# Mixture-of-experts blocks: adding a block's sums in steps between the next block's products, and the gather on both sides of the transposes

## The chip, the cores and the metric

The kernel runs on one core of a Trainium2 chip. The metric is the device time of one execution in microseconds (us). A core has a matrix engine (PE, with its weight loads PEld), a vector engine (DVE), an activation engine (ACT), a general engine (POOL), and SP, which here does little else than start DMA transfers. Each engine runs its own list of instructions in order; semaphores between them make one wait for another.

## The reference

Two layers, each a sequence mixer followed by a hierarchical mixture of experts (MoE) with 32 experts of 1024 x 1024 (gate and up) and 512 x 1024 (down) weights. All of it is in float32. What matters here is the MoE:

```python
def hier_moe(h, w_group, b_group, w_expert, b_expert, w_gate_up, w_down):
    g_logits = hf @ w_group + b_group                       # 4 groups
    g_sel = jnp.argmax(g_logits, -1)                        # top-1 group
    g_gate = take(softmax(g_logits), g_sel)
    e_logits = take((hf @ w_expert + b_expert).reshape(n_tok, 4, 8), g_sel)
    top_p, top_i = lax.top_k(jax.nn.softmax(e_logits, -1), 2)
    top_w = top_p / jnp.sum(top_p, -1, keepdims=True) * g_gate[:, None]
    # ... each (token, choice) goes to its expert e:
    def expert_block(args):
        xb, e = args
        gu = xb @ w_gate_up[e]                              # 1024 -> 2 x 512
        return (jax.nn.silu(gu[:, :512]) * gu[:, 512:]) @ w_down[e]   # 512 -> 1024
    return jnp.sum(out[dest].reshape(n_tok, 2, -1) * top_w[..., None], axis=1)

for i in range(2):                                          # layer 0: SSD mixer, layer 1: retention mixer
    x = layer_norm(ALPHA * x + g1 * (mixer(modulate(x)) @ out_w))     # layer 0: ctx the same way
    tokens = modulate(x, sh2, sc2)                          # layer 0: 256 latent + 256 context tokens; layer 1: 256
    ffn = hier_moe(tokens, ...)
    x = layer_norm(ALPHA * x + g2 * ffn)
```

Each MoE reads all 32 experts' weights once, 6 MB for each expert.

## The kernel before

The two mixers and the two MoEs follow each other. In a MoE (class `MoE`) every expert has a fixed number of slots for the tokens that chose it: 32, 64 or 96. Experts are worked off in blocks of 128 slots, by the loop in `pairs()`: a narrow block holds four experts of 32 slots, a wide one two of 64, a full one an expert of 96 and one of 32. Layer 0 (512 tokens, `nt` = 4 tiles of 128) has twelve blocks, here called p0 to p11: wide, wide, narrow, full, narrow, wide, wide, narrow, wide, wide, narrow, wide. Layer 1 (256 tokens, `nt` = 2) has ten. Blocks are grouped in twos for the gather.

For a block the loop issues, in this order, before the change:

- `gate_up`: for k = 0 to 7 the gate products (pg) and up products (pu) of each expert, L1839. An expert's tokens lie on 32 or 64 of PE's columns, so products of different experts stand side by side on the array (the rows show the tile as 128\*32 or 128\*64). Behind it tanh and two multiplications give th (L1844, L1848, L1849).
- `scatter_oh`: pb (L1809), from which DVE makes the one-hot matrix os that puts slots back to tokens.
- `ahead`: the block's share of the gather for the next group. One `part` is `gather` (px, L1778, 16 matmuls in layer 0 and 8 in layer 1, then copies into xT); each block of a group of two does two parts. The second block also does `weights`: `slot_w` (pw, L1794), the routing weight of each slot.
- `hidden_T`: four transposes of th (ph, L1856), copied to hT by ACT (L1858).
- `add`: the previous block's output is put back to tokens: for two halves u and `nt` token tiles two matmuls (pc, L1886), then DVE multiplies by the gate (L1911) and adds to the sum (L1912). That is 16 pc in layer 0 and 8 in layer 1, eight or four such steps.
- `down`: the down products (pd, L1868). `weighted` then scales them and splits them in two (ACT L1878, DVE L1879), which the next `add` reads.

Around p0 `ahead` stands behind `after` instead (LATE = 0). Behind block p5 in layer 0 and p4 in layer 1 (`REST`) the last block is added at once and `rest()` follows: a loop under `If` (L2087) over blocks for tokens beyond an expert's slots. Its count is zero for these inputs.

Inside an engine the order is not that of the code: these calls go through the framework's scheduler, which reorders matmuls of neighbouring steps where their data is there; so the pieces of order below are of the final programs. Weights come through a ring of 1 MB matrices in the pools A, B, E, F and X: `Ring.emit` (L175) starts a transfer (L186, on SP's queue) when the next matrix of a fixed plan finds a free slot, and a slot is free again when `done` has seen the last product that reads it, for a gate and up matrix behind every second k. SP issues strictly in the plan's order, so one slot that is late holds all later ones.

Of the kernel before, what the change touches and what calls it, by code (L numbers as in the profile page):

```python
# [27 lines left out]
EPS = 1e-5  # L28
LN = ("mix", "ffn")
REST = (5, 4)  # L30
FIXED, FULL = 4, 4

SLOTS = ([64] * 4 + [96] + [64] * 10 + [32] * 17, [32] * 4 + [96] + [64] * 6 + [32] * 21)
# [7 lines left out]
def const_layout():  # L41
# [3 lines left out]
    def add(name, a):  # L45
        parts.append((name, np.ascontiguousarray(a, dtype=np.float32)))

    add("ident", np.eye(128))
    add("r8", np.tile(np.arange(8, 0, -1), (128, 1)))
    add("i96", np.tile(np.arange(96), (128, 1)))  # L50
    add("s64", (i % 64)[:, None])
    e = np.arange(32)
# [157 lines left out]
def col(S, name, a=0, b=None):  # L210
    o, w = CL[name]
    return S.c[:, o + a:o + (w if b is None else b)]
# [1249 lines left out]
LATE = 0  # L1462
# [39 lines left out]
class MoE:  # L1502
# [397 lines left out]
            G.tensor_tensor(o, o, ln[:, 1024:], OP.add)  # L1900
        S.ring.done(("mix", self.layer))

    def add(self, os_, ys, n):
        V = self.S.nc.vector
        for u in range(2):
            for i in range(self.nt):
                pc = self.ps([P, 512], "pc", "cb")
                self.scattered(pc, os_, ys, n, i, u)
                c = slice(u * 512, (u + 1) * 512)
                t = self.wk2.tile([P, 512], F32, name="tl", bufs=2)  # L1910
                V.tensor_tensor(t, pc, self.gate(i)[:, c], OP.mult)  # L1911
                V.tensor_tensor(self.acc(i)[:, c], self.acc(i)[:, c], t, OP.add)  # L1912


    def pairs(self):
        S, order, groups = self.S, self.order, self.groups
        i96, s32, s64, s96 = (col(S, n) for n in ("i96", "s32", "s64", "s96"))
        xT, ws, G = {}, {}, self.G
        last = len(order) - 1

        def one_hots(g):
            runs = []
            for e in (e for p in groups[g] for e in order[p]):
                if runs and e == runs[-1][1] and self.slots(e) == self.slots(runs[-1][0]):
                    runs[-1][1] += 1
                else:
                    runs.append([e, e + 1])
            return self.gather_oh([(self.pos[:, :, a:b], self.slots(a)) for a, b in runs], i96)

        def weights(g):  # L1930
            for j, p in enumerate(groups[g]):
                ws[p] = self.slot_w(G[g], P * j, order[p])

        def start(g):
            for p in groups[g]:
                xT[p] = self.wk.tile([P, 8, P], F32, name="xT", bufs=3)

        def part(g, q, nb=2):
            self.gather(G[g], [xT[p] for p in groups[g]], q, nb)

        def ahead(p, g):
            own = groups[g - 1]
            for q in range(4)[slice(4 * own.index(p) // len(own), 4 * (own.index(p) + 1) // len(own))]:
                part(g, q)
            if p == own[-1]:
                weights(g)
        start(0)
        prev = None
        later = self.rest_of_route()

        def first(k):
            if k < 2 or k % 2 == 0:
                part(0, k if k < 2 else k // 2, 1 if k < 2 else 2)
            if k in ROUTE_K:
                next(later)

        def after(th, W, os_, w, end=False):
            nonlocal prev
            hT = self.hidden_T(th)
            if prev is not None:  # L1960
                self.add(*prev)
            pd = self.down(W, hT)
            prev = (os_, pd, w) if end else (os_, self.weighted(pd, w), 2)
        for p, places in enumerate(order):
            g = next(j for j, own in enumerate(groups) if p in own) + 1
            new = g < len(groups) and p == groups[g - 1][0]
            experts = {e: Expert(S, self.layer, e) for e in places}
            tiles = self.tiles_of(places)
            W = [(experts[e], w) for e, w in tiles]
            if new and p:  # L1970
                G[g] = one_hots(g)
            th = self.gate_up(W, xT[p], None if p else first)
            if p == 0:
                G[1] = one_hots(1)
                self.spread_rows()
            widths = [w for _, w in tiles]
            os_ = self.scatter_oh([(S.id2[:, e:e + 1], w) for e, w in tiles],
                                  s64 if widths[0] == 64 else s32 if len(experts) == 4 else s96)
            if g < len(groups):
                if p == 0:  # L1980
                    weights(0)
                    self.blocks()
                    self.base()
                if new:
                    start(g)
                if p > LATE:
                    ahead(p, g)
            after(th, W, os_, ws[p], p == last)
            if g < len(groups) and p <= LATE:
                ahead(p, g)  # L1990
            if p == REST[self.layer]:
                self.add(*prev)
                prev = None
                self.rest()
        return prev
# [286 lines left out]
```

## Time and profile before

| What | Value |
|---|---|
| runs, median (lowest to highest) | 2008.51 us (2006.31 to 2010.71), 3 runs |
| the profiled execution | 2005.95 us, span 2004.2 us |
| PE busy | 1769.8 us, 88% |
| PEld, DVE, ACT, POOL busy | 1002.5, 953.0, 489.4, 456.8 us |
| DMA moved | 543.84 MB, mean 271 GB/s |
| chain that ended last | DMA 8%, PE 2%, DVE 1% of the span |

The first MoE lies between about 620 and 1110 us, the second between about 1540 and 1985 us. In the page's forty slices the DMA engines' share is at 0.9 or more in most of these two stretches and much lower in the mixers, where PE is the busy engine. A window row gives, for a stretch from A to B in us, each engine's busy time with the count of instructions, the clock that PE was granted (1.00 is full), the mean share of time in which the core's DMA engines were busy, and what they moved; a share of 1.02 to 1.03 is what a full queue shows here. A timeline row gives start, duration, engine, line, operation, output and inputs by name, shape and count; in brackets is how long the engine had stood idle and what released it. A row of waits gives who waited for whom: total us, how many times, the longest. One float32 product shows as two passes in the timeline (x2).

### The profile page before, as it was taken

What the parts mean: (1) busy time and instruction counts of PE and PEld (TensorE: products, weight loads), DVE (VectorE), ACT (ScalarE), POOL (GpSimd) and SP (SyncE); (2) the same over time, 40 slices, a digit from 0 to 9 for tenths busy, and PEclk for the clock granted to TensorE, in tenths of its full rate; (3) what the DMA queues carried; (4) which work ended last, traced back from release to release, by engine and by line L of the source; (5) the groups of instructions that cost most, each with busy time, mean ns of one, the idle gap of its engine ahead of it and who ended that gap; (6) DMA issues with size and microseconds to landing.
All of it is one profiled execution on the core that took longest, in us unless ns stands there. A gap on an engine that the chain in (4) does not pass through costs nothing. (4 is left out here: it accounts for less than half of the span.)

```text
span 2004.2 us, 23517 instructions
## 1 busy us (share of the span) xinstructions
PE 1769.8 (88%) x9021; PEld 1002.5 (50%) x9021; DVE 953.0 (48%) x1685; ACT 489.4 (24%) x827; POOL 456.8 (23%) x275
## 2 busy tenths in 40 slices
PE   6899999999986999998999789988897998788886
PEld 3665666666764433332332488776873432123221
DVE  3847575765696434433243566474454432103112
ACT  2555454543212100000000233232232100000000
POOL 2343425343345000000000243454551100000000
PEclk8999999999997999999999899999997999989998
DMA  7423323336735999999999744474367999999996
GB/s 284 150 99 116 126 95 136 111 111 220 275 109 223 371 399 399 373 383 401 409 406 368 290 149 146 155 263 145 113 255 294 409 409 409 409 375 407 409 409 242
DMA packets 138022, 543.84 MB, mean 271 GB/s; under 512 B 10320, under 2 KB 10832, under 8 KB 125360
## 3 DMA queue, kind: packets, MB, share of 16 engines
q1 hardware_dynamic: 137328, 541.80, 69.9%
q8 instruction: 73, 1.20, 0.2%
q10 hardware_dynamic: 576, 0.48, 0.1%
q14 instruction: 45, 0.37, 0.0%
HBM read 537.00 MB, written 5.24 MB: 271 GB/s over the span
## 5 line engine op out<-in xcount | busy, mean ns | idle before, releaser
L441 POOL TENSOR_TENSOR wl<-ringA,wh 128x1024 fp32r<-128x1024 f32 x116 | 290.0, 2512 | 812.0 <-ACT wh L440 794.0
L440 ACT ACTIVATE wh<-ringA 128x1024 fp32r<-128x1024 f32 x118 | 124.3, 1058 | 225.5 <-PE pin L720 61.0
L720 PE MATMUL pin<-u,wh 128*128 128x512 f32 x304 | 132.0, 434 | 0.0
L1868 PE MATMUL pd<-ringB,hT 128*32 128x512 f32 (+1 forms) x472 | 123.0, 617 | 6.0 <-ACT hT L1858 4.5
L721 PE MATMUL pin<-u,wl 128*128 128x512 f32 x304 | 127.4, 419 | 0.0
L719 PE MATMUL pin<-u,wh 128*128 128x512 f32 x304 | 126.9, 417 | 0.0
L1879 DVE SCALAR_TENSOR_TENSOR yh<-pd,ws,yh 128x512 fp32r<-128x512 f32 x40 | 30.0, 751 | 198.1 <-ACT yh L1878 196.2
L1839 PE MATMUL pg<-ringE,xT 128*32 128x512 f32 (+1 forms) x312 | 110.4, 609 | 7.7 <-DMA ringE<-in_moe_w_gate_up_dram 7.2
L1839 PE MATMUL pu<-ringE,xT 128*32 128x512 f32 (+1 forms) x312 | 110.6, 609 | 3.6 <-DMA ringE<-in_moe_w_gate_up_dram 3.6
L1844 ACT ACTIVATE th<-pg 128x512 f32<-128x512 f32 x22 | 13.1, 597 | 402.9 <-PE pg L1839 392.8
L1848 DVE SCALAR_TENSOR_TENSOR th<-th,pg 128x512 f32<-128x512 f32 x22 | 15.1, 687 | 200.0 <-ACT th L1844 200.0
L750 DVE SCALAR_TENSOR_TENSOR cacc<-pad,cw,cacc 128x512 f32<-128x512 f32 x96 | 94.3, 986 | 13.6 <-ACT cacc L748 12.7
L2143 POOL TENSOR_TENSOR oacc<-oacc,ringX 128x512 f32<-128x512 f32 x1 | 1.6, 1623 | 432.6 <-ACT oacc L207 432.6
L1201 PE MATMUL pin<-u,wh 128*128 128x256 f32 (+1 forms) x256 | 84.9, 332 | 16.1 <-DVE gT L1253 10.0
L1911 DVE TENSOR_TENSOR tl<-pc,ringB 128x512 f32<-128x512 f32 x124 | 81.1, 685 | 37.1 <-PE pc L1886 35.3
L1839 PE MATMUL pg<-ringB,xT 128*32 128x512 f32 (+1 forms) x268 | 89.2, 613 | 5.9 <-DMA ringB<-in_moe_w_gate_up_dram 5.9
L1839 PE MATMUL pg<-ringA,xT 128*32 128x512 f32 (+1 forms) x244 | 85.7, 617 | 6.7 <-DMA ringA<-in_moe_w_gate_up_dram 6.2
L1778 PEld LDWEIGHTS px<-oh,hhl 128*128 128x128 f32 x576 | 73.3, 193 | 34.7 <-issue 32.2
L1839 PE MATMUL pu<-ringB,xT 128*32 128x512 f32 (+1 forms) x268 | 89.6, 609 | 0.9 <-DMA ringB<-in_moe_w_gate_up_dram 0.8
L1886 PE MATMUL pc<-yh,os 128*128 128x512 f32 x248 | 82.6, 432 | 8.0 <-DVE tl L1911 7.4
L1868 PE MATMUL pd<-ringE,hT 128*32 128x512 f32 (+1 forms) x240 | 77.1, 601 | 10.0 <-DMA ringE<-in_moe_w_down_dram 7.2
L1839 PE MATMUL pu<-ringA,xT 128*32 128x512 f32 (+1 forms) x244 | 83.1, 615 | 1.8 <-DMA ringA<-in_moe_w_gate_up_dram 1.8
(414 smaller groups left out, 3907.5 us busy)
## 6 DMA issues: line engine op xcount, KB each, us to landing
ringE<-in_moe_w_gate_up_dram SPq DMA_DIRECT2D x76, 1024.0 KB, 18.1
ringB<-in_moe_w_gate_up_dram SPq DMA_DIRECT2D x63, 1024.0 KB, 17.3
ringA<-in_moe_w_gate_up_dram SPq DMA_DIRECT2D x55, 1024.0 KB, 17.6
ringB<-in_moe_w_down_dram SPq DMA_DIRECT2D x53, 1024.0 KB, 18.0
ringA<-in_mod_w_dram SPq DMA_DIRECT2D x40, 1024.0 KB, 4.9
ringF<-in_moe_w_gate_up_dram SPq DMA_DIRECT2D x34, 1024.0 KB, 17.7
ringX<-in_moe_w_gate_up_dram SPq DMA_DIRECT2D x28, 1024.0 KB, 18.1
ringE<-in_moe_w_down_dram SPq DMA_DIRECT2D x28, 1024.0 KB, 18.2
```

The costliest lines, as they stand in the source:

```text
L440: S.split = nc.scalar.activation(hi, w, AF.Copy).ins
L441: (eng or nc.gpsimd).tensor_tensor(lo, w, hi.bitcast(F32), OP.subtract)
L719: S.nc.tensor.matmul(p, h, self.uh(k), start=k == 0, stop=False)
L720: S.nc.tensor.matmul(p, h, self.ul(k), start=False, stop=False)
L721: S.nc.tensor.matmul(p, l, self.uh(k), start=False, stop=k == 7)
L750: nc.vector.scalar_tensor_tensor(acc, pad[:, :, t:t + 256], cw[:, m, t:t + 1], acc, op0=OP.mult, op1=OP.add)
L1201: self.S.nc.tensor.matmul(p, a, self.uh(k)[:, T], start=k == 0, stop=False)
L1778: nc.tensor.matmul(px[:, b, :], self.S.hhl[i][:, m, j * 128:(j + 1) * 128], oh[:, i], start=i == 0 and m == 0, stop=i == nt - 1 and m == 1)
L1839: nc.tensor.matmul(po[o:o + n, :], xT[:, k, a:a + n], w.get(k)[:, u * 512:(u + 1) * 512], start=k == 0, stop=k == 7)
L1868: nc.tensor.matmul(pd[u % n][o:o + m, :], hT[:, j, a:a + m], w.get(8 + j)[:, u * 512:(u + 1) * 512], start=j == 0, stop=j == 3)
L1886: self.S.nc.tensor.matmul(pc, os_[s, i * 128:(i + 1) * 128], ys[q][s, u % n], start=q == 0, stop=q == 1)
L1911: V.tensor_tensor(t, pc, self.gate(i)[:, c], OP.mult)
```

## The change

`add` becomes a generator, `add_steps`, which stops behind every step. `gate_up` of the next block calls for one step ahead of each k from ADD_K = 1 on, and what is left is done behind it; `after` no longer adds. `ahead` becomes a generator too: one part of the gather is issued ahead of `hidden_T`, the rest of the block's share and `weights` between `hidden_T` and `down`. The add behind p5 (p4 in layer 1) and all of p0 stay. The program's lines move down by one up to the new function, so L1839 becomes L1840, L1886 L1887, L1868 L1869, L1778 L1779, L1794 L1795, L1856 L1857.

```diff
--- before.py
+++ after.py
@@ -28,6 +28,7 @@
 EPS = 1e-5
 LN = ("mix", "ffn")
 REST = (5, 4)
+ADD_K = 1
 FIXED, FULL = 4, 4
 
 SLOTS = ([64] * 4 + [96] + [64] * 10 + [32] * 17, [32] * 4 + [96] + [64] * 6 + [32] * 21)
@@ -1900,7 +1901,11 @@
             G.tensor_tensor(o, o, ln[:, 1024:], OP.add)
         S.ring.done(("mix", self.layer))
 
-    def add(self, os_, ys, n):
+    def add(self, *block):
+        for _ in self.add_steps(*block):
+            pass
+
+    def add_steps(self, os_, ys, n):
         V = self.S.nc.vector
         for u in range(2):
             for i in range(self.nt):
@@ -1910,6 +1915,7 @@
                 t = self.wk2.tile([P, 512], F32, name="tl", bufs=2)
                 V.tensor_tensor(t, pc, self.gate(i)[:, c], OP.mult)
                 V.tensor_tensor(self.acc(i)[:, c], self.acc(i)[:, c], t, OP.add)
+                yield
 
 
     def pairs(self):
@@ -1939,9 +1945,11 @@
             self.gather(G[g], [xT[p] for p in groups[g]], q, nb)
 
         def ahead(p, g):
+
             own = groups[g - 1]
             for q in range(4)[slice(4 * own.index(p) // len(own), 4 * (own.index(p) + 1) // len(own))]:
                 part(g, q)
+                yield
             if p == own[-1]:
                 weights(g)
         start(0)
@@ -1954,11 +1962,11 @@
             if k in ROUTE_K:
                 next(later)
 
-        def after(th, W, os_, w, end=False):
+        def after(th, W, os_, w, end, side):
             nonlocal prev
             hT = self.hidden_T(th)
-            if prev is not None:
-                self.add(*prev)
+            for _ in side:
+                pass
             pd = self.down(W, hT)
             prev = (os_, pd, w) if end else (os_, self.weighted(pd, w), 2)
         for p, places in enumerate(order):
@@ -1969,7 +1977,11 @@
             W = [(experts[e], w) for e, w in tiles]
             if new and p:
                 G[g] = one_hots(g)
-            th = self.gate_up(W, xT[p], None if p else first)
+
+            adding = self.add_steps(*prev) if prev is not None else iter(())
+            th = self.gate_up(W, xT[p], (lambda k: k >= ADD_K and next(adding, None)) if p else first)
+            for _ in adding:
+                pass
             if p == 0:
                 G[1] = one_hots(1)
                 self.spread_rows()
@@ -1983,11 +1995,13 @@
                     self.base()
                 if new:
                     start(g)
-                if p > LATE:
-                    ahead(p, g)
-            after(th, W, os_, ws[p], p == last)
-            if g < len(groups) and p <= LATE:
-                ahead(p, g)
+            side = ahead(p, g) if g < len(groups) else iter(())
+            if p > LATE:
+                next(side, None)
+            after(th, W, os_, ws[p], p == last, side if p > LATE else ())
+            if p <= LATE:
+                for _ in side:
+                    pass
             if p == REST[self.layer]:
                 self.add(*prev)
                 prev = None
```

In the final programs each engine has the same instructions; SP's and POOL's stand in the same order, PE's, DVE's and ACT's differ inside the two MoEs. Three places on PE, each before and then after.

First the end of p1 in layer 0: before, the gather for the next blocks (px), the routing weights (pw), the adds of p0 (pc), the transposes (ph) and p1's down products (pd, from ringF):

```order
L1778 MATMUL px<-oh,hhl 128x256 x32
L1794 MATMUL pw<-wr,oh 128x8 x4
L1886 MATMUL pc<-yh,os 128x512 x4
L1839 MATMUL pg<-ringB,xT 32x512
L1794 MATMUL pw<-wr,oh 128x56 x4
L1856 MATMUL ph<-c,th 128x128 x4
L1886 MATMUL pc<-yh,os 128x512 x4
L1868 MATMUL pd<-ringF,hT 64x512 x3
L1886 MATMUL pc<-yh,os 128x512 x4
L1868 MATMUL pd<-ringF,hT 64x512 x4
L1886 MATMUL pc<-yh,os 128x512 x4
L1868 MATMUL pd<-ringF,hT 64x512
```

After, from the last of p1's gate and up products on:

```order
L1840 MATMUL pg<-ringA,xT 64x512 x2
L1840 MATMUL pu<-ringA,xT 64x512 x2
L1887 MATMUL pc<-yh,os 128x512 x2
L1840 MATMUL pg<-ringA,xT 64x512 x2
L1840 MATMUL pu<-ringA,xT 64x512 x2
L1887 MATMUL pc<-yh,os 128x512 x2
...
L1779 MATMUL px<-oh,hhl 128x256 x16
L1840 MATMUL pg<-ringB,xT 32x512
L1857 MATMUL ph<-c,th 128x128 x4
L1779 MATMUL px<-oh,hhl 128x256 x16
L1795 MATMUL pw<-wr,oh 128x8 x4
L1869 MATMUL pd<-ringF,hT 64x512 x3
```

The adds have moved from both sides of the transposes into the k's; half of the px and all pw have moved behind the transposes, and pd is no longer mixed with pc.

Then p7, a narrow block, towards the end of its gate and up products before the change:

```order
L1778 MATMUL px<-oh,hhl 128x256 x24
L1794 MATMUL pw<-wr,oh 128x4 x4
L1886 MATMUL pc<-yh,os 128x512
L1839 MATMUL pg<-ringX,xT 32x512
L1839 MATMUL pu<-ringX,xT 32x512
...
L1886 MATMUL pc<-yh,os 128x512 x3
L1839 MATMUL pg<-ringE,xT 32x512
L1839 MATMUL pu<-ringE,xT 32x512
L1886 MATMUL pc<-yh,os 128x512 x5
L1839 MATMUL pg<-ringE,xT 32x512
L1839 MATMUL pu<-ringE,xT 32x512
L1886 MATMUL pc<-yh,os 128x512 x6
```

After, two of its first k's, and then its transposes and what follows them:

```order
L1887 MATMUL pc<-yh,os 128x512 x2
L1840 MATMUL pg<-ringA,xT 32x512 x2
L1840 MATMUL pg<-ringF,xT 32x512 x2
L1840 MATMUL pu<-ringA,xT 32x512 x2
L1840 MATMUL pu<-ringF,xT 32x512 x2
L1887 MATMUL pc<-yh,os 128x512 x2
...
L1857 MATMUL ph<-c,th 128x128 x4
L1779 MATMUL px<-oh,hhl 128x256 x16
L1795 MATMUL pw<-wr,oh 128x4 x4
L1869 MATMUL pd<-ringA,hT 32x512
L1795 MATMUL pw<-wr,oh 128x4 x4
```

Before, single experts' products stand between lots of pc; now pc stand in twos behind full k's of two and two products, and 16 px with pw stand behind ph.

Last p9, a wide block, from its transposes on; before:

```order
L1856 MATMUL ph<-c,th 128x128 x4
L1809 LDWEIGHTS id_98
L1809 MATMUL pb<-posT,id_98 32x512
...
L1868 MATMUL pd<-ringE,hT 64x512 x2
L1868 MATMUL pd<-ringA,hT 64x512 x2
L1868 MATMUL pd<-ringE,hT 64x512
L1868 MATMUL pd<-ringA,hT 64x512
L1868 MATMUL pd<-ringE,hT 64x512
```

After:

```order
L1857 MATMUL ph<-c,th 128x128 x4
L1779 MATMUL px<-oh,hhl 128x256 x16
L1795 MATMUL pw<-wr,oh 128x8 x4
L1869 MATMUL pd<-ringE,hT 64x512
L1869 MATMUL pd<-ringA,hT 64x512
L1869 MATMUL pd<-ringE,hT 64x512
L1795 MATMUL pw<-wr,oh 128x4 x4
L1869 MATMUL pd<-ringA,hT 64x512
```

Behind p9's transposes 16 px and pw have come, and pw's second half splits the pd; before, this block's gather stood in p8.

## Rows read from the trace of the kernel before

**Rows 1.** Windows: busy time of each engine, clock, DMA share, GB/s.
```profile
core 0: us, PE busy (x) PEld busy (x) DVE busy (x) ACT busy (x) POOL busy (x), PEclk, DMA share, GB/s
700.00:800.00 100.00, 93.60 (x559) 37.30 (x552) 39.40 (x75) 7.71 (x15) 0.00 (x0) 1.00 1.02 404
800.00:808.00 8.00, 7.67 (x65) 2.93 (x67) 4.29 (x7) 0.00 (x0) 0.00 (x0) 1.00 0.33 116
896.00:904.00 8.00, 8.00 (x39) 2.56 (x36) 0.42 (x1) 1.29 (x3) 0.00 (x0) 1.00 0.55 191
904.00:920.00 16.00, 11.06 (x56) 2.20 (x56) 1.50 (x2) 1.06 (x2) 0.00 (x0) 0.80 1.02 411
1056.00:1064.00 8.00, 8.00 (x63) 2.62 (x65) 3.04 (x5) 0.00 (x0) 0.00 (x0) 1.00 0.42 150
1772.00:1784.00 12.00, 10.47 (x45) 2.83 (x48) 0.71 (x1) 1.28 (x2) 0.00 (x0) 0.86 0.71 264
1784.00:1976.00 192.00, 166.81 (x761) 51.29 (x754) 36.27 (x66) 13.69 (x25) 0.00 (x0) 0.98 1.03 409
```

**Rows 2.** DMA issues on SP (start, us, queue, operation, tiles, count).
```profile
679.66 1.19 SPq L186 DMA_DIRECT2D ringA<-in_moe_w_gate_up_dram  x2
694.03 2.49 SPq L186 DMA_DIRECT2D ringF<-in_moe_w_gate_up_dram  x2
...
791.51 0.37 SPq L186 DMA_DIRECT2D ringX<-in_moe_w_gate_up_dram  x1
804.39 0.37 SPq L186 DMA_DIRECT2D ringE<-in_moe_w_gate_up_dram  x1
...
882.22 19.46 SPq L186 DMA_DIRECT2D ringF<-in_moe_w_gate_up_dram  x2
...
1047.72 13.42 SPq L186 DMA_DIRECT2D ringF<-in_moe_w_gate_up_dram  x2
1061.38 0.37 SPq L186 DMA_DIRECT2D ringB<-in_moe_w_down_dram  x1
```

**Rows 3.** Waits of SP at 785 to 810, 880 to 905, 1755 to 1785.
```profile
SPq L186 <- PE pu L1839: 13.8, 4, 12.3
...
SPq L2087 <- SPq L2087: 15.8, 5, 7.5
...
SPq L2087 <- SPq L2087: 15.5, 7, 2.6
```

**Rows 4.** Waits of PE, 655 to 905 (three), then 905 to 1075 (one).
```profile
PE pc L1886 <- DVE tl L1911: 3.4, 7, 1.1
PE pd L1868 <- ACT hT L1858: 2.0, 4, 0.7
PE pu L1839 <- DMA ringB<-in_moe_w_gate_up_dram: 0.8, 1, 0.8
...
PE pd L1868 <- ACT hT L1858: 1.7, 4, 0.4
```

**Rows 5.** Timeline of PE, single groups: start, us, line, operation, tiles, shape, count.
```profile
652.59 1.05 PE L1794 MATMUL pw<-wr,oh 128*128 128x4 f32 x8
...
736.21 3.49 PE L1778 MATMUL px<-oh,hhl 128*128 128x256 f32 x27
...
1048.50 1.05 PE L1839 MATMUL pg<-ringF,xT 128*32 128x512 f32 x2
1049.38 1.02 PE L1839 MATMUL pu<-ringF,xT 128*32 128x512 f32 x2
1050.33 1.20 PE L1886 MATMUL pc<-yh,os 128*128 128x512 f32 x4
```

**Rows 6.** Timeline of PE, a wait in p2.
```profile
743.70 0.61 PE L1794 MATMUL pw<-wr,oh 128*128 128x4 f32 x4 [1.03 <-DVE xT L1786]
```

**Rows 7.** Timeline in p7: PE's last wait for a DMA, ACT's tanh.
```profile
916.96 1.06 PE L1839 MATMUL pg<-ringB,xT 128*32 128x512 f32 x1 [0.64 <-DMA ringB<-in_moe_w_gate_up_dram]
...
948.93 0.60 ACT L1844 ACTIVATE th<-pg 128x512 f32<-128x512 f32 x1 [18.14 <-PE pg L1839]
```

## The prediction

> **What bounds the kernel now.** I read the windows of the two MoE stages first, then the DMA issues on SP where the DMA share falls, then what SP and PE wait for there, and last the single rows of PE. In the MoE stages the reader is to see the DMA share at 1.02 to 1.03 with about 409 GB/s while PE is busy for nine tenths [rows 1]: weights set the pace, and time is lost where the DMA queue runs dry. It does so four times. Against a share of 1.03 the row from 800 lacks (1.03 - 0.33) x 8 = 5.6 us, from 896 3.8 us, from 1056 4.9 us, from 1772 3.8 us [rows 1]; I call them dips 1 to 4.
>
> What makes them differs. Before dip 1 SP issues a matrix at 791.51 and the next at 804.39, and before dip 3 it stands from 1047.72 to 1061.38 [rows 2]; the wait is for gate and up products, 12.3 us the longest around dip 1 [rows 3]. The slot comes free with the second pair of steps (k = 1) of block p4's gate and up products, and of p10's. From 655 to 905 PE waits for a DMA once, 0.8 us [rows 4]: PE is late by its own work, and dip 1 is PE's. Dips 2 and 4 are of another kind: SP stands 15.8 and 15.5 us at L2087, the branch around the loop for left-over blocks, which runs zero times here [rows 3]; the last issue ahead of it is at 882.22 [rows 2]. The change touches neither that branch nor the order of SP's instructions, so these two stay.
>
> So a microsecond taken from PE ahead of p4's or p10's release is worth a microsecond until the dip is closed, 5.6 and 4.9 us at most; elsewhere it is worth nothing. What the DMA queue gives back reaches the end whole, since the queue is full again behind each dip.
>
> **Prices.** A gather matmul (px) is 3.49 / 27 = 0.13 us, sixteen are 2.1; the eight routing-weight matmuls (pw) take 1.05 us; a product of one expert alone on the array takes 0.88 us, from 1048.50 to 1049.38, as long as four experts side by side, so what counts is the number of steps; and between narrow products and a full-width matmul lie 1050.33 - 1049.38 - 0.88 = 0.07 us, which I take as 0.09 with the way back; an add matmul (pc) is 1.20 / 4 = 0.30 us [rows 5]. The change adds and removes no instruction; it moves them.
>
> **Up to p4's release (dip 1).** In p1 the adds of p0 stood behind the transposes and among the down products, and now stand in pairs behind each k of p1's gate and up products (first piece). Counted over the blocks p1 to p4, the order has 97 steps of narrow products before and 94 after, since lone experts now find partners: 3 x 0.88 = 2.6 us less. Of the gather, 16 px that stood ahead of the release now stand behind p4's transposes: 2.1 us less. Between narrow and full-width there are 31 changes where there were 26: 5 x 0.09 = 0.45 us more. That is -4.2 us. pc and pw number the same on both sides.
>
> Waits: the second part of the gather now stands between the transposes and the down products, so PE works while ACT copies hT. Of the four waits for hT that make 2.0 us [rows 4] the longest, 0.7, is p5's; the others are (2.0 - 0.7) / 3 = 0.43 us, and p2's and p3's go. So do the 1.03 us that pw waited for a copy of xT in p2 [rows 6], as down products now stand between the two halves of pw: -1.9 us. The add's own waits (3.4 us in seven [rows 4]) may shrink where adds stand apart; I cost that at nothing. The sum is -6.1 us, against 5.6 us of dip: it closes, with 0.5 us in hand. If the pw wait came back (it is covered by only three down products) it would be -5.1, and 0.5 us of the dip would stay. What the adds delay in p1 is the release of its gate matrices, 0.60 + 0.09 us more with each k, some 4.8 us with the last of seven; the queue holds enough for that: SP's next issue but one comes only at 694.03 after 679.66 [rows 2], and the down products that free its slot have the same work ahead of them as before. That cover is thin, as the queue is all but empty at 694; if it fails, dip 1 begins there and its gain shrinks by as much.
>
> On changes of width the trace shows the 0.07 us above. The Trainium skill, "TensorEngine Tiling (Array Packing)", section Tiling Modes, says that a change of tiling mode drains TensorE, which speaks against a change that adds such switches. If each of the five new ones cost half a step, 0.44 us, the switches would cost 2.2 us instead of 0.45 and the sum would be -4.3 us: dip 1 would keep 1.3 us. No row here shows a drain that long.
>
> **p5, ahead of dip 2.** 16 px and pw that stood in p4 now stand behind p5's transposes: 3.1 us, less the 0.7 us that its down products waited for hT. SP waits at the branch for landings meanwhile, and that is what hides it; without that cover it would cost the 2.4 us. In p6, 16 px move from one side of the transposes to the other.
>
> **From p6 to p10's release (dip 3).** In p7 the second piece shows 16 px and the adds crowded behind the last products, each lone expert between two lots of adds; now the adds stand in pairs in the first k's, where PE waits for DMA anyway (for the last time 0.64 us at 916.96 [rows 7]). Ahead of p7's transposes this takes 16 px (2.1), pw (1.05) and 6 steps of 34 (5.3): -8.4 us. It can't be more than the DMA lets it: eight more matrices at 2.56 us each (1 MB at 409 GB/s) land after 916.96, the last at about 937.4, and four steps follow: 940.9 against the tanh at 948.93 [rows 7], so -8.0 us at most, and I take that. From there to p10's release the order has 96 steps in both. The third piece shows p9's 16 px and pw, which stood in p8 before: with p7's and p8's shifts, 2.1 + 1.05 us come in; the waits for hT (1.7 us in four [rows 4]) go in p7, p8 and p9, 1.3 us. Together -8.0 + 3.1 - 1.3 = -6.2 us against 4.9 us: dip 3 closes, with 1.3 us in hand. Should p7 give only half, it is -2.2 us, and 2.7 of the dip stay.
>
> **Layer 1.** The same moves with half as many px and pc (two token tiles), but the stage is at 1.03 from 1784 on [rows 1], and its one dip is SP's branch. I cost it at nothing, between -1 and +1 us.
>
> **Sum.** -5.6 - 4.9 = -10.5 us. The profiled execution is 2005.95 us (span 2004.2), which gives 1995.5; it lies 2.6 us below the median of the runs, 2008.51, and from that the forecast is 1998.0 us.
>
> **Rivals.**
> - Only dip 1 closes. For it: dip 3 hangs on p7, where PE's granted clock fell when it waited for DMA (the window from 904 has it at 0.80 [rows 1]), and PE will wait there still. Against it: half of p7's gain would do for half the dip. It gives 2008.5 - 5.6 = 2002.9.
> - No change: the order already had the adds of p2 to p4 mixed into the next block's products in both kernels, so the change does less than it says, and SP's release could turn out to hang on something other than those steps. Against it: the counts above are of the final order. 2008.5.
> - More: SP reaches the branch with fewer transfers outstanding, and dips 2 and 4 close too: another 7.6 us, 1990.4. Against it: the last landing sets that wait, and it moves along with the rest.
> - Slower: the adds between the k's hold the gate matrices' slots longer, in p1, p2 and p7, up to 4.8 us in each, and the queue has nothing to cover it. Each microsecond then is a lost transfer. It decides from where the delays that aren't covered pass the 10.5 us that the dips give; with all three in full it is 14.4 - 10.5 = +3.9 us, 2012.4, and more if a dip stays open as well. For it: the empty queue at 694. Against it: in p7 those steps wait for DMA themselves.
>
> **Chances and range.** Both close 0.53, only dip 1 0.20, no change 0.12, more 0.08, slower 0.07. About 0.2%, 4 us, is what a measurement here can tell from no change. Of the slower case I count most above that bound; with the first, second and fourth case faster is 0.81, same 0.13, slower 0.06. The range from 1994 to 2005 takes in partly closed dips and an error in the prices of 4 us below; it leaves out the no-change and slower cases, and the case of more.
>
> **What would show it.** Right: no window in 790 to 810 or 1040 to 1065 with a share under 0.95; SP's issue behind p4's and p10's k = 1 about 6 us earlier, relative to the queue; dips at the branch as before; PE waiting for DMA now and then in p4 and p10. Wrong: a gap in SP's issues in p1 near 690, a DMA share under 1 between 675 and 700, or p7's tanh less than 4 us earlier relative to the branch. If dips 1 and 3 are gone and the time isn't lower, the claim that lost DMA time reaches the end is the one that failed.

## The result, and the profile after

The changed kernel takes 1998.15 us (median of 5 runs, 1996.14 to 1999.17) against 2008.51 us before (5 runs, 2006.31 to 2012.44): ratio 0.9943, 95% interval 0.9929 to 0.9957. That is 10.4 us less, and between 8.6 and 14.3 by the interval. The forecast of 1998.0 us was right, and so was the view that dips 1 and 3 close. How the parts add up was not as forecast.

| | before | after |
|---|---|---|
| profiled execution, span | 2005.95, 2004.2 us | 1998.15, 1996.4 us |
| PE, DVE, ACT busy | 1769.8, 953.0, 489.4 us | 1769.1, 957.7, 489.6 us |
| DMA mean | 271 GB/s | 272 GB/s |

No engine has less work; what is gone is, in the main, time in which the DMA queue was empty. Windows of the profile after, with the columns of [rows 1]:

```profile
core 0: us, PE busy (x) PEld busy (x) DVE busy (x) ACT busy (x) POOL busy (x), PEclk, DMA share, GB/s
694.00:702.00 8.00, 8.00 (x42) 3.55 (x42) 3.38 (x17) 0.38 (x1) 0.00 (x0) 1.00 0.68 240
794.00:808.00 14.00, 13.67 (x106) 5.20 (x106) 5.79 (x10) 0.00 (x0) 0.00 (x0) 1.00 1.03 410
895.00:903.00 8.00, 8.00 (x47) 4.26 (x48) 0.42 (x1) 0.98 (x2) 0.00 (x0) 1.00 0.39 144
1040.00:1064.00 24.00, 22.33 (x139) 7.24 (x136) 9.86 (x17) 0.60 (x1) 0.00 (x0) 1.00 1.03 409
1764.00:1776.00 12.00, 9.49 (x50) 2.41 (x46) 2.79 (x4) 1.27 (x2) 0.00 (x0) 0.86 0.68 258
```

The rows from 794 and 1040 answer to those from 800 and 1056 in [rows 1]: the share is 1.03, dips 1 and 3 are gone. The rows from 895 and 1764 are dips 2 and 4: (1.03 - 0.39) x 8 = 5.1 us where 3.8 stood, and 4.2 where 3.8 stood. The first row is new: from 694 to 702 the queue lacks 0.35 x 8 = 2.8 us. Before, the same stretch reads (first row here; the second belongs to the last section)

```profile
694.00:702.00 8.00, 8.00 (x46) 2.73 (x50) 6.25 (x16) 1.37 (x2) 0.00 (x0) 1.00 1.01 352
994.00:1000.00 6.00, 5.36 (x15) 1.81 (x16) 1.16 (x3) 0.60 (x1) 0.00 (x0) 0.72 1.03 410
```

with a share of 1.01. SP's DMA issues of the profile after show the same three places:

```profile
688.11 0.99 SPq L187 DMA_DIRECT2D ringA<-in_moe_w_gate_up_dram  x2
699.34 1.22 SPq L187 DMA_DIRECT2D ringF<-in_moe_w_gate_up_dram  x2
...
787.99 0.37 SPq L187 DMA_DIRECT2D ringX<-in_moe_w_gate_up_dram  x1
800.72 0.37 SPq L187 DMA_DIRECT2D ringE<-in_moe_w_gate_up_dram  x1
...
1038.19 13.44 SPq L187 DMA_DIRECT2D ringF<-in_moe_w_gate_up_dram  x2
1051.87 0.37 SPq L187 DMA_DIRECT2D ringB<-in_moe_w_down_dram  x1
```

The pairs at 787.99 and 800.72 and at 1038.19 and 1051.87 are as far apart as in [rows 2]: SP still waits for p4's and p10's release, but the queue is not empty when it comes. The new gap is at 688.11 to 699.34. In [rows 2] the second of these stood at 694.03; p0's tanh, from which the MoE may be counted, came 2.3 us later in this execution than before (654.14 against 651.85, below), so the issue is 694.03 - 699.34 + 2.3 = -3.0, that is 3.0 us late. What SP waited for longest from 670 to 706, before and then after:

```profile
SPq L186 <- PE pd L1868: 16.7, 4, 13.0
...
SPq L187 <- PE pd L1869: 12.5, 4, 10.0
```

In both a down product releases this issue. Waits after, PE from 655 to 905, then SP at the branch:

```profile
PE pc L1887 <- DVE tl L1916: 2.6, 5, 1.1
PE pg L1840 <- SPq L2101: 1.6, 1, 1.6
PE pd L1869 <- DMA ringA<-in_moe_w_down_dram: 0.6, 1, 0.6
...
SPq L2101 <- SPq L2101: 16.5, 5, 8.4
```

Against [rows 4], pd no longer waits for hT in this stretch and pc's waits went from 3.4 to 2.6 us. New are 0.6 us for the landing of a down matrix and 1.6 us in which PE waits for SP's branch, and the branch takes 16.5 us where it took 15.8 [rows 3].

### The profile page after: what moved, and what is told of

The parts are those of the page before. It is cut to its first block, busy times and chain, and to the rows that moved or that the text cites. A ratio compares the mean times of both kernels' runs of the same rounds, so it can differ in the third digit from the quotient of the medians.

```text
span 1996.4 us, 23495 instructions
## 1 busy us (share of the span) xinstructions
PE 1769.1 (89%) x9021; PEld 1002.2 (50%) x9021; DVE 957.7 (48%) x1685; ACT 489.6 (25%) x827; POOL 456.6 (23%) x275
## 5 line engine op out<-in xcount | busy, mean ns | idle before, releaser
L1869 PE MATMUL pd<-ringB,hT 128*32 128x512 f32 (+1 forms) x472 | 123.6, 626 | 3.1 <-DMA ringB<-in_moe_w_down_dram 2.0
L1840 PE MATMUL pg<-ringE,xT 128*32 128x512 f32 (+1 forms) x312 | 109.5, 613 | 9.5 <-DMA ringE<-in_moe_w_gate_up_dram 9.2
L1840 PE MATMUL pu<-ringE,xT 128*32 128x512 f32 (+1 forms) x312 | 109.8, 609 | 3.6 <-DMA ringE<-in_moe_w_gate_up_dram 3.6
L1202 PE MATMUL pin<-u,wh 128*128 128x256 f32 (+1 forms) x256 | 84.2, 330 | 15.2 <-DVE gT L1254 10.2
L1840 PE MATMUL pg<-ringB,xT 128*32 128x512 f32 (+1 forms) x268 | 87.2, 609 | 8.1 <-DMA ringB<-in_moe_w_gate_up_dram 7.5
L1887 PE MATMUL pc<-yh,os 128*128 128x512 f32 x248 | 83.3, 435 | 6.7 <-DVE tl L1916 3.7
L1840 PE MATMUL pu<-ringB,xT 128*32 128x512 f32 (+1 forms) x268 | 87.0, 609 | 0.1
L1779 PE MATMUL px<-oh,hhl 128*128 128x256 f32 (+1 forms) x576 | 86.1, 294 | 0.2 <-ACT ringX L1573 0.2
L1779 PEld LDWEIGHTS px<-oh,hhl 128*128 128x128 f32 x576 | 75.0, 193 | 21.8 <-issue 17.4
L1840 PE MATMUL pg<-ringA,xT 128*32 128x512 f32 (+1 forms) x244 | 78.9, 611 | 5.0 <-DMA ringA<-in_moe_w_gate_up_dram 2.8
L1203 PE MATMUL pin<-u,wh 128*128 128x256 f32 (+1 forms) x256 | 83.1, 325 | 0.1
## 6 DMA issues: line engine op xcount, KB each, us to landing
ringE<-in_moe_w_gate_up_dram SPq DMA_DIRECT2D x76, 1024.0 KB, 18.2
ringB<-in_moe_w_down_dram SPq DMA_DIRECT2D x53, 1024.0 KB, 18.3
```

The costliest lines, as they stand in the source:

```text
L1202: self.S.nc.tensor.matmul(p, a, self.uh(k)[:, T], start=k == 0, stop=False)
L1203: self.S.nc.tensor.matmul(p, a, self.ul(k)[:, T], start=False, stop=False)
L1779: nc.tensor.matmul(px[:, b, :], self.S.hhl[i][:, m, j * 128:(j + 1) * 128], oh[:, i], start=i == 0 and m == 0, stop=i == nt - 1 and m == 1)
L1840: nc.tensor.matmul(po[o:o + n, :], xT[:, k, a:a + n], w.get(k)[:, u * 512:(u + 1) * 512], start=k == 0, stop=k == 7)
L1869: nc.tensor.matmul(pd[u % n][o:o + m, :], hT[:, j, a:a + m], w.get(8 + j)[:, u * 512:(u + 1) * 512], start=j == 0, stop=j == 3)
L1887: self.S.nc.tensor.matmul(pc, os_[s, i * 128:(i + 1) * 128], ys[q][s, u % n], start=q == 0, stop=q == 1)
```

## The experiments

Medians and ratios to the kernel before, which ran on the same chip beside it (2008.51 us beside the changed kernel, 2008.28 beside the next four, 2007.14 beside the last three, 2008.12 beside those run once more); gap and dips are (1.03 - share) x width, in us, of windows at the places named above (dip 4 is 3.8 to 4.4 in all that have the branch).

| kernel | us | ratio, 95% interval | gap in p1 | dip 1 | dip 2 | dip 3 |
|---|---|---|---|---|---|---|
| before | 2008.51 | | 0.2 | 5.6 | 3.8 | 4.9 |
| changed | 1998.15 | 0.9943 [0.9929, 0.9957] | 2.8 | 0 | 5.1 | 0 |
| adds_only | 2003.96 | 0.9974 [0.9965, 0.9983] | 7.1 | 3.8 | 3.9 | 0.2 |
| gather_only | 1994.82 | 0.9939 [0.9922, 0.9955] | 0.4 | 0.8 | 4.2 | 0.2 |
| p1_back | 1995.63 | 0.9936 [0.9921, 0.9952] | 0.4 | 0 | 4.7 | 0 |
| p7_back | 1996.95 | 0.9943 [0.9929, 0.9956] | 2.8 | 0.1 | 4.9 | 0 |
| p1_back_px | 1996.11 | 0.9946 [0.9930, 0.9961] | 0.6 | 3.3 | 3.8 | 0.2 |
| before_norest | 1997.35 | 0.9951 [0.9934, 0.9968] | 0.5 | 5.0 | 0.1 | 0.3 |
| p1_back_norest | 1987.16 | 0.9898 [0.9884, 0.9913] | 0.5 | 0.1 | 0.1 | 0 |

**The two halves of the change apart.** `adds_only` keeps the adds between the k's and does the whole share of the gather ahead of the transposes:

```diff
             if p > LATE:
-                next(side, None)
-            after(th, W, os_, ws[p], p == last, side if p > LATE else ())
+                for _ in side:
+                    pass
+            after(th, W, os_, ws[p], p == last, ())
```

> The adds between the k's as in the changed kernel, the whole gather share and pw ahead of the transposes as before. Theory (PE's release of p4's and p10's gate slots sets the time; adds in p1 hold its gate slots): PE is ahead of before by only 1.3 us at p4 and the waits for hT stay, the dip near 697 is there (about 2.8 us), so dip 1 is not gone but smaller by 1.3 plus those 2.8, net gain there 1 to 2 us; in p7 3.4 us of lone steps go, dip 3 keeps 1 to 2 us. Time 2003 to 2005 (ratio about 0.998). Rival (the adds are the whole change, the gather's place is indifferent): the same as the changed kernel, 1998.

```profile
694.00:706.00 12.00, 11.74 (x57) 3.79 (x51) 3.33 (x17) 1.09 (x2) 0.00 (x0) 1.00 0.44 152
804.00:812.00 8.00, 7.68 (x57) 2.92 (x57) 5.06 (x9) 0.00 (x0) 0.00 (x0) 1.00 0.55 187
1040.00:1064.00 24.00, 23.64 (x120) 8.39 (x120) 11.37 (x18) 1.37 (x2) 0.00 (x0) 1.00 1.02 405
```

The ratio is the theory's, the split is not: the gap in p1 is 7.1 us, more than twice the changed kernel's, and dip 1 is still at 3.8; dip 3 is closed. PE reaches p4's tanh 166.9 us behind p0's, 4.0 later than before (162.8) where the theory had 1.3 earlier. The issue behind the gap comes at 702.90, 49.5 us behind p0's tanh (653.43) against 42.2 before: 7.3 us late for a gap of 7.1, as 3.0 us late made 2.8 above. And the ratio came out right for a reason that I can't show: gap and dips add up to 15.0 us against 14.5 before, and from p0's tanh to p11's this kernel takes 459.9 us against 461.7 and 459.8 in the two profiles of before, yet its median is 4.3 us lower. `gather_only` is the other half:

```diff
-            adding = self.add_steps(*prev) if prev is not None else iter(())
-            th = self.gate_up(W, xT[p], (lambda k: ...) if p else first)
-            for _ in adding:
-                pass
+            th = self.gate_up(W, xT[p], None if p else first)
...
             hT = self.hidden_T(th)
+            if prev is not None:
+                self.add(*prev)
             for _ in side:
                 pass
```

> The gather on both sides of the transposes, the adds behind the transposes as before. Theory: PE is 4.1 us of work and some 2 us of waits ahead at p4's release, no gap near 697, so dip 1 closes whole (5.6 us); p7's lone steps stay, so dip 3 keeps about 4 of its 4.9 us. Time 2001 to 2003 (ratio 0.997). Rival (adds are the whole change): 2008, ratio 1.000. Rival (the gather is the whole change): 1998.

```profile
694.00:702.00 8.00, 8.00 (x48) 2.66 (x50) 5.51 (x18) 1.38 (x2) 0.00 (x0) 1.00 1.00 388
796.00:806.00 10.00, 9.67 (x87) 3.77 (x90) 3.90 (x7) 0.00 (x0) 0.00 (x0) 1.00 0.95 366
1040.00:1064.00 24.00, 22.03 (x142) 7.76 (x141) 9.62 (x16) 1.14 (x2) 0.00 (x0) 1.00 1.02 407
```

Faster than expected (the theory had 2001 to 2003), and by the medians faster than the changed kernel: no gap in p1, dip 1 at 0.8 us, and dip 3 closed as well, which the theory had kept open. SP's issues in p1 are those of before:

```profile
680.90 1.19 SPq L187 DMA_DIRECT2D ringA<-in_moe_w_gate_up_dram  x2
695.32 1.21 SPq L187 DMA_DIRECT2D ringF<-in_moe_w_gate_up_dram  x2
```

695.32 less 680.90 is 14.4 us, as 694.03 less 679.66 in [rows 2]; after the change it was 11.2 from a first issue that itself came late. So the gather's new place closes the dips without the adds, and the gap in p1 is there only in the kernels with the adds between the k's.

**The adds of p1 alone put back.** In `p1_back` only block p1 of layer 0 adds behind its transposes, as before:

```diff
+            later_add = self.layer == 0 and p in (1,)
-            th = self.gate_up(..., (lambda k: k >= ADD_K and next(adding, None)) ...)
-            for _ in adding:
+            th = self.gate_up(..., (lambda k: k >= ADD_K and not later_add and next(adding, None)) ...)
+            for _ in () if later_add else adding:
...
             hT = self.hidden_T(th)
+            for _ in adding:
+                pass
```

> The changed kernel, but in block p1 of layer 0 the adds stand behind the transposes again. Theory: the gap of 2.8 us at 696 to 702, which the adds in p1 made by holding its gate slots, is gone, dip 1 stays closed (PE is 1 us further ahead than in the changed kernel): 2.5 us faster than the changed kernel, 1995 to 1996, ratio to before 0.993. Rival (the new gap is not the adds' doing, or what it costs is given back at dip 1): 1998 as the changed kernel, with the gap still there or a dip of the same size at 800.

```profile
694.00:702.00 8.00, 8.00 (x46) 2.58 (x46) 5.81 (x22) 1.38 (x2) 0.00 (x0) 1.00 1.00 361
790.00:806.00 16.00, 15.67 (x124) 6.05 (x124) 5.45 (x9) 0.00 (x0) 0.00 (x0) 1.00 1.03 409
```

The gap is gone and dip 1 stays closed. The gap was the doing of those sixteen matmuls' new place.

**The adds of p7 alone put back.** `p7_back` is the same edit with p in (7,).

> The changed kernel, but in block p7 of layer 0 the adds stand behind the transposes again. Theory: 3.3 us more on PE ahead of p10's release, less than 2 us of it in hand, so dip 3 opens again with 1.5 to 4 us, dip 1 stays closed: 2000 to 2002, ratio 0.996. Rival (dip 3 closed because of the gather parts alone, or with everything from the branch on shifted): dip 3 stays closed, 1998.

```profile
1040.00:1062.00 22.00, 21.59 (x138) 7.45 (x136) 8.81 (x15) 0.60 (x1) 0.00 (x0) 1.00 1.03 409
```

Here the theory fell: dip 3 stays closed, at 1.03 from 1040 to 1062, and the time is not longer than the changed kernel's. p7's adds were not needed for it. The tanh of p6, p7 and p10 in this kernel:

```profile
887.77 0.60 ACT L1845 ACTIVATE th<-pg 128x512 f32<-128x512 f32 x1 [21.17 <-PE pg L1840]
...
940.51 0.60 ACT L1845 ACTIVATE th<-pg 128x512 f32<-128x512 f32 x1 [15.31 <-PE pg L1840]
...
1061.10 0.60 ACT L1845 ACTIVATE th<-pg 128x512 f32<-128x512 f32 x1 [23.21 <-PE pg L1840]
```

**More work for PE ahead of p4's release.** In `p1_back_px` block p3's gather is done three times.

```diff
-                part(g, q)
+                for _ in range(3 if self.layer == 0 and p == 3 else 1):
+                    part(g, q)
```

> The kernel of p1_back (1995.6 us) with the gather matmuls of block p3 in layer 0 made three times instead of once: 64 px more, 8.2 us, of which some 7.3 stand ahead of p4's release. Theory: the release has about 2 us in hand in p1_back (p0's to p4's tanh is 7.9 us shorter than before, the dip 5.6), so the first 2 us cost nothing and the rest opens dip 1 again with 5 to 5.5 us: 2000.5 to 2001.5, and the time moves by as much as the dip. Rival (PE's work costs its own time wherever it stands): 2003 to 2004. Rival (dip 1 is not PE's): no dip, 1995 to 1996.

```profile
796.00:804.00 8.00, 8.00 (x54) 2.73 (x57) 5.56 (x9) 0.38 (x1) 0.00 (x0) 1.00 0.62 218
```

Dip 1 is back with (1.03 - 0.62) x 8 = 3.3 us: PE makes it. It is smaller than expected. From p0's tanh to p4's the profile has 159.9 us against 154.9 in p1_back, so 5.0 of the 7.3 us came through and 1.7 us of them cost nothing. PE's idle time in that stretch fell by only 0.8 us (4.2 to 3.4), so waits took up little of the rest; the other products must have taken less in their new order, which I have not taken apart. The medians are 0.5 us apart where the theory had 5 to 6, and the intervals overlap, so the runs alone can't settle what the dip costs. The first MoE can: from p0's tanh to p11's it takes 453.0 us against 450.2 and 450.4 in the two profiles of p1_back, so 2.7 to 2.8 us more with dip 1 larger by 3.3 and dip 2 smaller by 0.9. The 8.2 us of work cost less than 3 us there, so PE's work does not cost its own time wherever it stands.

**Without the branch.** `before_norest` and `p1_back_norest` leave out the call of `rest()`, so the loop for tokens beyond an expert's slots isn't there; these inputs have none, others may.

```diff
                 self.add(*prev)
                 prev = None
-                self.rest()
```

> The kernel before without the call of rest(): the empty loop for left-over blocks and its branch are gone in both layers (a loop that runs zero times with these inputs). Theory (dips 2 and 4 are SP waiting for all its transfers at the branch): both dips go, 3.9 and 4.0 us; PE has the same work, so p10's release may come no earlier and dip 3 may grow by what dip 2 gave back: between 4 and 8 us faster, 2000 to 2004. Rival (these dips are PE's down products, which free the slots late): the dips stay, 2008.

```profile
800.00:808.00 8.00, 7.68 (x67) 2.90 (x68) 4.29 (x7) 0.00 (x0) 0.00 (x0) 1.00 0.40 157
896.00:904.00 8.00, 6.01 (x26) 2.00 (x24) 2.70 (x5) 1.19 (x2) 0.00 (x0) 1.00 1.03 410
926.00:932.00 6.00, 6.00 (x51) 1.97 (x50) 3.50 (x11) 0.00 (x0) 0.00 (x0) 1.00 0.73 264
1050.00:1066.00 16.00, 14.65 (x127) 5.55 (x126) 4.37 (x7) 0.60 (x1) 0.00 (x0) 1.00 1.01 400
```

The rows from 800 and 1050 are dips 1 and 3, that from 896 is where dip 2 was. Dip 2 is gone, so it was the branch's; dip 1 is as it was, and 1.8 us appear at 926 to 932. Dip 3 closed too (0.3 us), which the theory did not ask for, and the median of 1997.35 us lies below the theory's 2000; PE's order in p6 and p7 is another one without the loop between them, and I have not taken that apart.

> The kernel of p1_back (1995.6 us) without the call of rest(). Theory: all four dips gone, 4.7 and 4 us less: 1987 to 1988, faster than both kernels and than the kernel before without rest(), as PE is ahead. Rival (with the queue full everywhere PE is what is late next): dips come back elsewhere in p6 to p10, 1991 to 1995.

```profile
880.00:912.00 32.00, 30.02 (x136) 12.77 (x133) 10.39 (x19) 3.34 (x6) 0.00 (x0) 1.00 1.03 409
1040.00:1062.00 22.00, 19.64 (x139) 6.64 (x138) 4.97 (x8) 1.20 (x2) 0.00 (x0) 1.00 1.03 409
1750.00:1786.00 36.00, 30.71 (x125) 7.94 (x122) 6.38 (x10) 1.38 (x2) 0.00 (x0) 1.00 1.03 410
1102.00:1110.00 8.00, 7.76 (x29) 2.84 (x31) 0.00 (x0) 0.18 (x1) 0.00 (x0) 0.79 0.62 243
```

All four are closed: the first three rows are the stretches of dips 2, 3 and 4. At 1102 to 1110 there is another of 3.3 us, in p11, with PE's granted clock at 0.79. It is not this kernel's own: the changed kernel has one of 2.5 us at the same distance from p11's tanh (2.2 in its second profile), where the profiles of before have 1.0 to 1.1.

```profile
1112.00:1118.00 6.00, 6.00 (x26) 2.20 (x24) 0.00 (x0) 0.00 (x0) 0.00 (x0) 0.85 0.62 238
```

The last section comes back to it. At 1987.16 us this is the fastest kernel of the study, but it does less than the others. Among those with all the work `gather_only` and `p1_back` have the lowest medians.

**Once more.** A second profile of the kernel before; then the changed kernel beside the two that seemed faster, these three on one chip.

> The kernel before once more, for a second profile. Theory: dips at the same four places with the same sizes within 0.5 us; the granted clock's fall in p8 (994 to 1000) and the time between the MoEs differ from execution to execution by 2 to 3 us. Rival: the fall of the clock in p8 belongs to this order of work and is there again.

```profile
802.00:810.00 8.00, 7.69 (x65) 2.97 (x67) 4.29 (x7) 0.00 (x0) 0.00 (x0) 1.00 0.42 151
898.00:906.00 8.00, 8.00 (x38) 2.54 (x36) 0.42 (x1) 1.31 (x3) 0.00 (x0) 1.00 0.59 198
1056.00:1064.00 8.00, 8.00 (x62) 2.70 (x64) 3.27 (x6) 0.00 (x0) 0.00 (x0) 1.00 0.58 208
994.00:1000.00 6.00, 4.01 (x15) 1.38 (x15) 2.70 (x5) 0.84 (x2) 0.00 (x0) 1.00 1.03 410
```

Everything lies 2 us later here (p0's tanh is at 653.89). Dips 1 to 3 are there again, with 4.9, 3.5 and 3.6 us: dip 1 and dip 3 were 0.7 and 1.3 us larger in the first profile, more than I expected. The last row is for the last section.

> The changed kernel once more, on the same chip as the two that follow. Theory: the gap near 697 (2.8 us) is there in this profile too, dips 1 and 3 closed; ratio to before 0.994 to 0.995. Rival (the gap was one execution's): no gap.

```profile
696.00:704.00 8.00, 8.00 (x38) 2.73 (x39) 3.00 (x15) 0.81 (x2) 0.00 (x0) 1.00 0.70 252
```

(1.03 - 0.70) x 8 = 2.6 us: the gap belongs to the kernel. Its median is 1998.31 us, ratio 0.9947 [0.9934, 0.9961].

> The kernel of gather_only once more, beside the changed kernel. Theory: 2 to 3 us faster than the changed kernel, as it lacks the gap near 697 and keeps dips 1 and 3 closed to within 1 us. Rival (the adds between the k's give something in p7 or in layer 1 that makes up for the gap): the same time as the changed kernel within 1 us.

1994.98 us, ratio 0.9929 [0.9916, 0.9943]: 3.3 us faster than the changed kernel beside it, about as the theory says, though the two intervals overlap.

> The kernel of p1_back once more, beside the two. Theory: as gather_again within 1 us, 2 to 3 us faster than the changed kernel: the adds elsewhere cost and give nothing. Rival: 1 us or more faster than gather_again, so the adds in p2 and p7 do give something.

1995.55 us, ratio 0.9937 [0.9924, 0.9951], which lies between the two; whether the adds in p2 and p7 give anything can't be told from these. The first MoE, p0's tanh to p11's, differs less between profiles of one kernel: 452.4 us in both of the changed kernel, 450.2 and 450.4 in p1_back, 450.6 and 451.5 in gather_only. Putting p1's adds back is worth 2.0 to 2.2 us there, most of the gap's 2.6 to 2.8.

## Why the prediction was right, point by point

Starts of ACT's tanh in blocks p0, p4, p6, p10 and p11, before and then (with p7 as well) after:

```profile
651.85 0.60 ACT L1844 ACTIVATE th<-pg 128x512 f32<-128x512 f32 x1 [2.90 <-PE pg L1839]
...
814.69 0.60 ACT L1844 ACTIVATE th<-pg 128x512 f32<-128x512 f32 x1 [21.64 <-PE pg L1839]
...
891.70 0.60 ACT L1844 ACTIVATE th<-pg 128x512 f32<-128x512 f32 x1 [23.05 <-PE pg L1839]
...
1071.06 0.60 ACT L1844 ACTIVATE th<-pg 128x512 f32<-128x512 f32 x1 [23.20 <-PE pg L1839]
...
1113.56 0.60 ACT L1844 ACTIVATE th<-pg 128x512 f32<-128x512 f32 x1 [21.66 <-PE pg L1839]
```

```profile
654.14 0.60 ACT L1845 ACTIVATE th<-pg 128x512 f32<-128x512 f32 x1 [2.90 <-PE pg L1840]
...
811.02 0.60 ACT L1845 ACTIVATE th<-pg 128x512 f32<-128x512 f32 x1 [20.73 <-PE pg L1840]
...
889.99 0.60 ACT L1845 ACTIVATE th<-pg 128x512 f32<-128x512 f32 x1 [21.18 <-PE pg L1840]
...
939.55 0.60 ACT L1845 ACTIVATE th<-pg 128x512 f32<-128x512 f32 x1 [3.81 <-PE pg L1840]
...
1062.40 0.60 ACT L1845 ACTIVATE th<-pg 128x512 f32<-128x512 f32 x1 [24.06 <-PE pg L1840]
...
1106.58 0.60 ACT L1845 ACTIVATE th<-pg 128x512 f32<-128x512 f32 x1 [21.67 <-PE pg L1840]
```

**PE's gain up to p4: right.** From p0's tanh to p4's there are 162.8 us before and 156.9 after: -6.0 (162.84 and 156.88) against the sum of -6.1. That the sum took the waits for hT at nothing left and the pw wait as gone agrees with the waits after. The gain is the gather's: gather_only has 157.1 us, -5.8. The adds cost some 2 us of it in p1 (154.9 in p1_back) and give some 2 us in p2 to p4 (154.9 against 157.1). The rule of the Trainium skill, "TensorEngine Tiling (Array Packing)", section Tiling Modes, would with an assumed half step for each change of mode have made it -4.3; the measured -6.0 is nearer to the sum with the 0.09 us of the row, though no run measures a change of mode by itself.

**Dip 1 gives 5.6 us: half wrong.** The step that failed is "the queue holds enough for that: ... the down products that free its slot have the same work ahead of them as before". The adds in p1 move the issue at 694.03 back by 3.0 us; the queue had nothing left there, as the text said, and 2.8 us (2.6 in the second profile) were lost at 697. p1_back shows that the adds of this one block do it. The work ahead is not the same: in the first order piece twelve pc stand ahead of the seventh pd before, and after the change all sixteen do. Four pc are 1.2 us at the 0.30 of [rows 5]; the other 1.8 I have not taken apart. The late release of the gate matrices, which the text priced at 4.8 us, did no harm by itself: SP's issue at 688.11 is 6.1 us late against 679.66 + 2.3, and the share stays at 1.03 from 675 to 694. So dip 1 gave 5.6 - 2.8 = 2.8 us net. The prediction named the place and the sign, "a gap in SP's issues in p1 near 690", and this sign of being wrong came true; in the sum it had a price of nothing.

**Dips 2 and 4 stay: right**, and before_norest shows that dip 2 is the branch. But dip 2 grew by 1.3 us, in gather_only by 0.4 and in p1_back by 0.9. The 1.6 us that PE waits there is p7's first product, which the order puts ahead of p6's transposes; that wait lies inside the branch's. The second profiles have 3.5 before and 5.1 after. Why the last landings before the branch take longer (18.2 us from issue to landing before, 19.5 after) I have not settled.

**p7 gains 8.0 us: right in size.** From p6's tanh to p7's, 57.2 us before (891.70 to 948.93 in [rows 7]) and 49.6 after: -7.7. From there to p10's tanh 122.1 and 122.9: +0.7 where the text had +1.8. Against the second profile of before, 120.6 us, it is +2.3; in the first the clock fell in p8 (last section).

**Dip 3 needs p7: wrong.** "Should p7 give only half, it is -2.2 us, and 2.7 of the dip stay" fell with p7_back: p7 gives 4.5 us there (887.77 to 940.51, 52.7 us), and the dip is closed. From p6's tanh to p10's there are 179.4 us before, 172.4 after and 173.3 in p7_back. Either half of the change closes dip 3 (0.2 us in adds_only and in gather_only). The term that failed is the +1.8 us from p7 to p10, which the text added to the half gain too: with p7 later that stretch is 120.6 us against 122.9 in the changed kernel, and as long as in the second profile of before. PE waits for DMA twice in it in the changed kernel, 1.2 us, and not in p7_back; the other 1.1 us I have not taken apart. And the dip to be closed was 3.6 us in the second profile of before, not 4.9. Against that profile p6 to p10 is 177.6 - 173.3 = 4.3 us shorter in p7_back, enough for 3.6.

**Layer 1 gives nothing: right.** Dip 4 is 3.8 before and 4.2 after (4.0 in both second profiles), and from the first tanh of that stage to the last there are 418.5 us before and 418.7 after.

**The sum.** Dips and gap of the first MoE fall by 5.6 + 4.9 - 2.8 - 1.3 = 6.4 us by the profiles, not 10.5. Counted from p0's tanh to p11's the first MoE is 461.7 us before (459.8 in the second profile), 452.4 after in both: 7.4 to 9.3 us less. The medians differ by 10.4. That lost DMA time reaches the end of this MoE holds over all thirteen profiles: summed in windows of 2 us with a share below 0.97, from 22 us behind p0's tanh to p11's, the queue loses some 15 and 13 us before, 8 in both after, 5 in both of p1_back and less than 1 in p1_back_norest, and p0 to p11 less this sum is 444 to 447 us in every one, while p0 to p11 itself runs from 445.7 to 461.7. Within that band before lies at 446 to 447 and the changed kernel at 444 to 445, so some 2 us of its gain are not in the dips. What the median fell by beyond the first MoE no run shows. The stretch between the two MoEs, which the change does not touch, differs by several us between executions of one kernel (430.3 and 435.7 us in the two of gather_only), so part of the agreement with 1998.0 is luck: two terms were too large by some 4 us together, and what made up for them was not in the sum. Of the rivals, "slower" came nearest to what went wrong: the adds do delay a release that nothing covers, but it is a down matrix's, in one block and with 2.8 us, not that of gate matrices in three with 4.8.

## What to carry to other kernels

When a full DMA queue sets the time, read how much is queued at every place where the order moves work ahead of a release, not only at the places where the queue runs dry now: a gain at one dip can be spent at the next thin spot. Moving half the gather and the weights behind the transposes, where a copy was waited for anyway and, in p4, behind the release, gave all that the whole change gave; which of these moves counts most no run separates. Without the other half of the change the first MoE is 0.9 to 1.9 us shorter still. And an empty branch at which SP waits for its outstanding transfers cost a dip of its own at both places where it stands here, 3.8 us each, and both dips are gone without it.

## What the runs showed of the hardware

In the first profile of before PE's granted clock was 0.72 in the mean from 994 to 1000 (0.50 from 996 to 998, the lower of its two levels, 1.2 GHz), behind the waits of p8's transposes and down products; in the second it was 1.00 in the same stretch with the same program (the rows from 994 above). PE was busy for 5.36 us of that stretch in the first and 4.01 in the second, and dip 3, which comes next, was 4.9 and 3.6 us. p11 shows it too. Behind its tanh PE waits for the transposes and for hT, and in four of the eleven profiles with the branch (both of the changed kernel, p7_back, the second of gather_only) the clock then falls to 0.50 as the down products begin: in the changed kernel it is 0.57 in the mean from 1110 to 1114, and the DMA share falls right behind (the row from 1112 above). From p11's tanh to SP's issue of the next layer's router weights there are 19.9 to 20.0 us in these four and 18.3 in the other seven, so the fall costs 1.7 us; gather_only has one profile of each kind. A single profile can hold a fall of the clock to its lower level that belongs to the execution and not to the kernel, and a sum that rests on a dip behind it inherits that error.

Before the branch the last transfer's tail is uneven: in windows of 1 us the DMA share goes from full to nothing over 2 to 3 us rather than at once (before: 0.98, 0.49, 0.25 and 0.00 from 897 to 901). I take part of dip 2 to be this tail; no run separates it from the wait behind it.
